# Padding the two rings of split weights by 64 and 96 bytes a buffer in a two-layer encoder kernel

## The chip, the cores and the metric

The kernel runs on one core of one Trainium2 chip. The metric is the device time of one execution in microseconds (us). Before the change three runs gave a median of 1837.78 us (1837.69 to 1837.85).

## The reference, cut to what matters

Two layers over 256 frames of width 1024, all in float32. Each layer has a mixer (layer 0: latent attention, "mla"; layer 1: sparse attention with a top-k indexer, "dsa"), a layer norm, an expert channel mixer ("peer") and another layer norm. Nearly all of the arithmetic is in the peer part: of 16384 experts it needs, for each frame, the product with their down rows, a gelu, a gate, and the sum of their up rows.

```python
def per_block(args):
    x_blk, e_blk, g_blk = args
    u = w_down[e_blk]
    a = jnp.einsum('td,ted->te', x_blk, u).astype(jnp.float32)
    hg = (jax.nn.gelu(a, approximate=False) * g_blk).astype(w_up.dtype)
    return jnp.einsum('te,ted->td', hg, w_up[e_blk]).astype(x_blk.dtype)
...
for i in range(DEPTH):
    m = _mla_mixer(...) if i % N_MIXERS == 0 else _dsa_mixer(...)
    x = _layernorm(DN_ALPHA * x + m, ln_gain[i, 0], ln_bias[i, 0])
    f = _peer(x, peer_w_q[i], peer_sub_keys[i], peer_w_down[i], peer_w_up[i])
    x = _layernorm(DN_ALPHA * x + f, ln_gain[i, 1], ln_bias[i, 1])
```

## The kernel before

The kernel doesn't gather experts. It multiplies the frames with the down rows of all 16384 experts, sets a gate that is zero for those not chosen, and multiplies with all up rows. So the weights go through the core once, as 128x1024 float32 blocks (4096 bytes in each of the 128 partitions). `Stream` (L52 to L131) feeds them: SyncE's queue loads a block into one of four `raw` buffers (L77), ScalarE copies it, rounded to float32r, into one of four `hi` buffers (L96), and VectorE writes the remainder raw - hi, float32r too, into one of four `lo` buffers (L100; a few on GpSimd, L98). `open` and `close` (L110 to L127) do the same with the subtraction set later, and `first` (L1142) does block 0 by hand with `hi0` and `lo0` from L1133 and L1134. `get` keeps three blocks split ahead of the one in use, and three more loaded.

The frames are split in the same way into `xh` and `xl` (128 x 8 x 256 float32r each). Every product of a frame chunk with a weight chunk is three float32r matmuls, high by high, low by high and high by low (`mm3`, L258). TensorE is the only engine that does them, all at L253 (`mm`). An operand that stands still in the array is loaded ahead of each matmul (LDWEIGHTS, "PEld" in the profile), while the one before still runs; the other operand moves through it. Three shapes matter here:

- **256 columns, weights stand still** (`proj`, L264): the group `d` (the peer's down product, twice 128 blocks of 24 matmuls), `pq` (the peer's queries), `q` and `qi` (dsa's), `h`, `krope` and `kn` (mla's). The weights are a slice of 128 columns (512 bytes) of a hi or lo buffer, and a 256-column chunk (1024 bytes) of `xh` or `xl` moves.
- **512 columns, weights move** (`rows`, L289): the group `y` (the peer's up product, twice 128 blocks of 12 matmuls, and the output projections), `v` and `qw`. Half of a hi or lo buffer (2048 bytes) moves, a slice of 128 columns of `xh` or `xl` stands still.
- **the exceptions**: `qn` and `qr` of mla (`up`, L745) move a 256-column float32r piece that lies in the tiles `V` and `U` (L721, L725) instead of `xh` and `xl`, and `ki` of dsa (L832) loads slices of only 72 columns, 288 bytes apart, from one hi and one lo buffer.

While the down product runs, VectorE, ScalarE and GpSimd choose the experts (`choose`, from L995) and build the gates (L1053 to L1059), and TensorE puts small matmuls `G` (L1068) between the blocks. The order on each engine comes from the order of the code and a scheduler.

SBUF is laid out by the order in which pools are opened (L167 to L176): `lead`, `wide` (xh, xl), `raws`, `his`, `los`, `big` (the arena), `const`, `small`, `ohp` (V and U). In the program as built, the first bytes of the buffers in each partition are, before:

| buffers | first byte | past a multiple of 512 |
|---|---|---|
| xh, xl | 17408, 25600 | 0, 0 |
| raw, four | 33792, 37888, 41984, 46080 | 0 |
| hi, four | 50176, 54272, 58368, 62464 | 0 |
| lo, four | 66560, 70656, 74752, 78848 | 0 |
| arena | 82944 | 0 |
| V, two; U, two | 220352, 222400; 224448, 226496 | 192 |

Of the kernel before, what the change touches and what calls it, by code (L numbers as in the profile page):

```python
# [11 lines left out]
F32R = mybir.dt.float32r  # L12
# [6 lines left out]
P = 128  # L19
T = 256  # L20
D = 1024
# [23 lines left out]
WARM = 9  # L45
EARLY = 11264
GSCALE = 2.0 ** 14
DSA_POOL = 3
MAGIC = 12582912.0


class Stream:  # L52
# [13 lines left out]

    def add(self, src, w=D):
        self.blocks += [(src[i], w) for i in range(src.shape[0])]

    def _load(self, upto):  # L70
        while self.n_loaded <= min(upto, len(self.blocks) - 1):
            src, w = self.blocks[self.n_loaded]
            if self.n_loaded in self.early:
                t = self.early[self.n_loaded]
            else:
                t = self.raw.tile([P, D], F32, tag="raw", name=f"raw{self.n_loaded}")
                self.last = self.nc.sync.dma_start(t[:, :w], src).ins  # L77
            self.tiles.append(t)
            self.n_loaded += 1
# [8 lines left out]
    def _split(self, upto, pooled=False):  # L88
        nc = self.nc
        while self.n_split <= min(upto, len(self.blocks) - 1):  # L90
            w = self.blocks[self.n_split][1]
            self._load(self.n_split)
            raw = self.tiles[self.n_split][:, :w]
            hi = self.hi.tile([P, D], F32R, tag="hi", name=f"hi{self.n_split}")[:, :w]
            lo = self.lo.tile([P, D], F32R, tag="lo", name=f"lo{self.n_split}")[:, :w]
            self.act(lambda: nc.scalar.copy(hi, raw))  # L96
            if pooled or self.share and self.n_split % self.share == 0:
                nc.gpsimd.tensor_tensor(lo, raw, hi.bitcast(F32), op=ALU.subtract)  # L98
            else:
                self.dve(lambda: nc.vector.tensor_tensor(lo, raw, hi.bitcast(F32), op=ALU.subtract))  # L100
            self.ready.append((hi, lo))
            self.n_split += 1
# [7 lines left out]
    def open(self, queue):  # L110

        i = self.n_split
        assert i == self.n_taken
        self._load(i)
        raw = self.tiles[i]
        hi = self.hi.tile([P, D], F32R, tag="hi", name=f"hi{i}")
        lo = self.lo.tile([P, D], F32R, tag="lo", name=f"lo{i}")
        queue("act", lambda: self.nc.scalar.copy(hi, raw))
        self.ready.append((hi, lo))
        self.n_split += 1  # L120
        self.n_taken += 1
        return i
# [39 lines left out]
def tile_trunk(ctx: ExitStack, tc: tile.TileContext, ins, out: bass.AP):  # L162
    nc = tc.nc
    def pool(name, bufs, **kw):
        return ctx.enter_context(tc.tile_pool(name=name, bufs=bufs, **kw))
# [4 lines left out]
    his = pool("his", 4)  # L170
    los = pool("los", 4)
# [41 lines left out]
    ws = Stream(nc, raws, his, los)  # L213
# [593 lines left out]
    def dsa():  # L807
# [82 lines left out]
        for t in range(2):  # L890
            for n in range(2):
                nc.scalar.copy(v[:, t, n * 512 : (n + 1) * 512], v4[t][n])
        ws.share = DSA_POOL
        for h in range(0, HEADS, 2):
# [22 lines left out]
    def peer(li):  # L917
# [77 lines left out]
        def choose():  # L995
# [40 lines left out]
            gt, i1 = tail[:, 0:T], tail[:, T : 2 * T]  # L1036
            nc.vector.tensor_scalar(gt, pg[:, :T], GSCALE, None, op0=ALU.mult)
            nc.vector.tensor_copy(gate16, gt)
# [23 lines left out]
        def place(g4, done):  # L1062
# [8 lines left out]
            if done < P:  # L1071
                nc.scalar.mul(A[:, done:, tsl], pv[:, done:, :], 1.0 / GSCALE)
            if done:
                nc.vector.scalar_tensor_tensor(A[:, :done, tsl], pv[:, :done, :], 1.0 / GSCALE, A[:, :done, tsl],
                                               op0=ALU.mult, op1=ALU.mult)
# [54 lines left out]
    xt = Arena(arena, 30720).take(NC, T)  # L1130
    piece = [slice(c, c + 2) for c in range(0, NC, 2)]
    raw0 = raws.tile([P, D], F32, tag="raw", name="raw0")
    hi0 = his.tile([P, D], F32R, tag="hi", name="hi0")  # L1133
    lo0 = los.tile([P, D], F32R, tag="lo", name="lo0")  # L1134
    nc.sync.dma_start(raw0, ins["mla_h"][0])
    for c in range(0, NC, 4):
        last = nc.sync.dma_start(xt[:, c : c + 4, :], ins["xT"][c // 4])
# [135 lines left out]
```

## Time and profile before

The profiled execution has a span of 1836.6 us; around it lie 1.2 us to the median of the runs.

| what | value |
|---|---|
| median of three runs | 1837.78 us |
| span of the profiled execution | 1836.6 us |
| mean granted TensorE clock | 0.999 |
| TensorE busy (matmuls) | 1824.8 us, 99% |
| VectorE, ScalarE, GpSimd busy | 1317.8, 1056.2, 362.8 us |
| moved by DMA | 335.47 MB, mean 183 GB/s |

A busy row of TensorE counts a matmul from its start until its result has left the array, so rows of neighbouring matmuls overlap: the mean ns of one matmul is longer than the distance between two starts. That distance (the pitch, below) is what the time is made of, and it is read from the chain of work that ended last (a piece's time by its count) or from starts in the order of time.

### The profile page before, as it was taken

Reading aid. Unit: us, or ns where it says so; the run is one execution under the profiler, and the core shown is the slowest. Engines: PE = TensorE matmul, PEld = TensorE weight load, DVE = VectorE, ACT = ScalarE, POOL = GpSimd, SP = SyncE. Lnnn points to the kernel's source line nnn. Section 1 sums busy time; section 2 is a strip of 40 time slices with the busy share of each in tenths; the row PEclk is TensorE's granted clock in tenths of the full one; section 3 lists DMA queues with packets and bytes.
Section 4 is the critical chain, followed back from the end, with each engine's and each line's share of the span. In section 5 each row is a group of like instructions: output and inputs, shape, how many; then the busy total and the mean of one; then the engine's idle time right before and its main releaser. Section 6 shows DMA issues by size and latency. Waiting matters only on the chain.

```text
span 1836.6 us, 32394 instructions
## 1 busy us (share of the span) xinstructions
PE 1824.8 (99%) x12495; PEld 1671.9 (91%) x12495; DVE 1317.8 (72%) x2348; ACT 1056.2 (58%) x1834; POOL 362.8 (20%) x265
## 2 busy tenths in 40 slices
PE   9999999999999999999999999999999999999998
PEld 8899999999998888888889899999999988888886
DVE  6689986788865555555688789957888765555555
ACT  6655456887764444444466555548877654444443
POOL 2002442445510000000022004504455300000000
PEclk9999999999999999999999999999999999999999
DMA  7554555444456555555646445554444475555553
GB/s 240 195 179 167 184 184 172 162 161 152 161 174 237 192 192 194 193 194 195 210 157 227 164 165 182 173 193 161 154 157 155 168 235 192 194 193 194 195 195 116
DMA packets 93468, 335.47 MB, mean 183 GB/s; under 512 B 10368, under 2 KB 11392, under 8 KB 93312
## 3 DMA queue, kind: packets, MB, share of 16 engines
q1 hardware_dynamic: 93024, 332.87, 52.9%
q8 instruction: 98, 1.61, 0.4%
q14 instruction: 58, 0.48, 0.1%
q10 hardware_dynamic: 288, 0.52, 0.1%
HBM read 329.16 MB, written 4.19 MB: 182 GB/s over the span
## 4 chain that ended last, share of the span: by engine, by line
PE 98%; DVE 1%; issue 1%; ACT 0%; DMA 0%; SPq 0%; DVEq 0%; POOLq 0%; POOL 0%; ACTq 0%
PE d L253 40%; PE y L253 40%; PE pq L253 4%; PE G L253 3%; PE q L253 3%; PE v L253 1%; PE qw L253 1%; PE s L253 1%; PE ps L253 1%; PE h L253 1%; PE qi L253 1%; PE o L253 1%; PE qn L253 0%; DMA arena<-in_xT 0%; PE kn L253 0%
## 5 line engine op out<-in xcount | busy, mean ns | idle before, releaser
L100 DVE TENSOR_TENSOR lo<-raw,hi 128x1024 fp32r<-128x1024 f32 (+1 forms) x579 | 763.9, 1321 | 345.0 <-ACT hi L96 344.1
L96 ACT CAST hi<-raw 128x1024 fp32r<-128x1024 f32 (+1 forms) x583 | 611.0, 1049 | 561.7 <-PE d L253 265.3
L253 PE MATMUL d<-xh,hi 128*128 128x256 f32 x2048 | 585.1, 286 | 0.0
L253 PE MATMUL d<-xh,lo 128*128 128x256 f32 x2048 | 579.2, 283 | 0.0
L253 PE MATMUL d<-xl,hi 128*128 128x256 f32 x2048 | 579.2, 283 | 0.0
L253 PEld LDWEIGHTS d<-xl,hi 128*128 128x128 f32 x2048 | 392.7, 192 | 0.0
L253 PEld LDWEIGHTS d<-xh,lo 128*128 128x128 f32 x2048 | 392.6, 192 | 0.0
L253 PEld LDWEIGHTS d<-xh,hi 128*128 128x128 f32 x2048 | 392.5, 192 | 0.0
L253 PE MATMUL y<-lo,xh 128*128 128x512 f32 x1088 | 337.7, 389 | 0.0
L253 PE MATMUL y<-hi,xh 128*128 128x512 f32 x1088 | 337.7, 390 | 0.0
L253 PE MATMUL y<-hi,xl 128*128 128x512 f32 x1088 | 337.3, 389 | 0.0
L1055 POOL TENSOR_TENSOR gate<-hot,gate 128x512 f16<-128x512 f16 x128 | 221.8, 1751 | 310.6 <-DVE hot L1053 310.6
L253 PEld LDWEIGHTS y<-lo,xh 128*128 128x128 f32 x1088 | 204.2, 188 | 42.7 <-DVE lo L100 0.3
L253 PEld LDWEIGHTS y<-hi,xl 128*128 128x128 f32 x1088 | 204.2, 188 | 42.4
L253 PEld LDWEIGHTS y<-hi,xh 128*128 128x128 f32 x1088 | 203.8, 188 | 41.8
L347 POOL TENSOR_TENSOR st<-st,mhalf 128x1 f32<-128x1 f32 x8 | 4.4, 551 | 827.2 <-DVE st L345 827.2
L1059 ACT ACTIVATE gate<-hot,rest 128x128 f16<-128x128 f16 x512 | 166.1, 413 | 0.9 <-DVE hot L1053 0.9
L1114 ACT CAST xh<-arena 128x512 fp32r<-128x512 f32 x128 | 79.8, 623 | 145.6 <-PE y L253 145.4
L1115 DVE TENSOR_TENSOR xl<-arena,xh 128x512 fp32r<-128x512 f32 x128 | 88.2, 692 | 73.5 <-ACT xh L1114 73.5
L1053 DVE TENSOR_TENSOR hot<-iota,place 128x1024 f16<-128x1024 f16 x128 | 84.9, 703 | 49.1 <-PE G L253 49.0
L1024 POOL TENSOR_TENSOR arena<-arena 128x800 f32<-128x800 f16 x32 | 78.8, 2482 | 38.8 <-DVE arena L1022 38.0
L253 PE MATMUL G<-gate,hot 128*128 128x128 f16 x1024 | 70.1, 221 | 0.0
(222 smaller groups left out, 1739.5 us busy)
## 6 DMA issues: line engine op xcount, KB each, us to landing
raw<-in_down SPq DMA_DIRECT2D x256, 512.0 KB, 3.2
raw<-in_up SPq DMA_DIRECT2D x256, 512.0 KB, 4.3
raw<-in_peer_q SPq DMA_DIRECT2D x24, 512.0 KB, 4.4
raw<-in_dsa_qk SPq DMA_DIRECT2D x16, 512.0 KB, 3.2
raw<-in_mla_w_o SPq DMA_DIRECT2D x8, 512.0 KB, 5.9
arena<-in_peer_q SPq DMA_DIRECT2D x8, 512.0 KB, 4.3
raw<-in_dsa_v SPq DMA_DIRECT2D x8, 512.0 KB, 4.3
raw<-in_dsa_w_o SPq DMA_DIRECT2D x8, 512.0 KB, 3.7
```

Source lines behind the costliest of these rows:

```text
L96: self.act(lambda: nc.scalar.copy(hi, raw))
L100: self.dve(lambda: nc.vector.tensor_tensor(lo, raw, hi.bitcast(F32), op=ALU.subtract))
L253: return pe(lambda: nc.tensor.matmul(o, l, r, start=start, stop=stop, skip_group_check=True))
L347: nc.gpsimd.tensor_tensor(st[:, 5:6], st[:, 4:5], mhalf, op=ALU.pow)
L1024: nc.gpsimd.tensor_tensor(o.rearrange("p k c -> p c k"), same, cell[t][:, h, :, None].to_broadcast([P, CELLS, TOPK]), op=ALU.mult)
L1053: nc.vector.tensor_tensor(hot, iota4[:, None].to_broadcast([P, 2, P, 4]), place16[:, :, None, four].to_broadcast([P, 2, P, 4]), op=ALU.is_ ...
L1055: nc.gpsimd.tensor_tensor(gate[:, 0], hot[:, 1].rearrange("p c j -> p j c"), gate16[:, four, None].to_broadcast([P, 4, P]), op=ALU.mult)
L1059: nc.scalar.mul(gate[:, 1, j, :], hot[:, 1, :, j], rest[:, t : t + 1])
L1114: nc.scalar.copy(hh, a)
L1115: nc.vector.tensor_tensor(al, a, hh.bitcast(F32), op=ALU.subtract)
```

## The change

Each buffer of the hi ring gets 16 more float32 columns (64 bytes), each of the lo ring 24 (96 bytes). The code uses the first 1024 columns only. `parts` allots both in one place for the three places that did so apart.

```diff
+HI_PAD, LO_PAD = 16, 24
...
+    def parts(self, i, w=D):
+
+        hi = self.hi.tile([P, D + HI_PAD], F32R, tag="hi", name=f"hi{i}")
+        lo = self.lo.tile([P, D + LO_PAD], F32R, tag="lo", name=f"lo{i}")
+        return hi[:, :w], lo[:, :w]
...
-            hi = self.hi.tile([P, D], F32R, tag="hi", name=f"hi{self.n_split}")[:, :w]
-            lo = self.lo.tile([P, D], F32R, tag="lo", name=f"lo{self.n_split}")[:, :w]
+            hi, lo = self.parts(self.n_split, w)
...
-        hi = self.hi.tile([P, D], F32R, tag="hi", name=f"hi{i}")
-        lo = self.lo.tile([P, D], F32R, tag="lo", name=f"lo{i}")
+        hi, lo = self.parts(i)
...
-    hi0 = his.tile([P, D], F32R, tag="hi", name="hi0")
-    lo0 = los.tile([P, D], F32R, tag="lo", name="lo0")
+    hi0, lo0 = ws.parts(0)
```

On every engine the instructions stand in the same order as before, row for row, with the same waits. Only addresses move:

| buffers | first byte after | past a multiple of 512 |
|---|---|---|
| xh, xl, raw | as before | 0 |
| hi, four | 50176, 54336, 58496, 62656 | 0, 64, 128, 192 |
| lo, four | 66816, 71008, 75200, 79392 | 256, 352, 448, 32 |
| arena | 83584 | 128 |
| V, two; U, two | 220992, 223040; 225088, 227136 | 320 |

## The prediction

> **What bounds the kernel now.** I read the page first: its busy times, the granted clock and the chain of work that ended last.
>
> ```profile
> PE 1824.8 (99%) x12495; PEld 1671.9 (91%) x12495; DVE 1317.8 (72%) x2348; ACT 1056.2 (58%) x1834; POOL 362.8 (20%) x265
> ...
> PEclk9999999999999999999999999999999999999999
> ...
> PE 98%; DVE 1%; issue 1%; ACT 0%; DMA 0%; SPq 0%; DVEq 0%; POOLq 0%; POOL 0%; ACTq 0%
> ```
>
> 98% of the chain is TensorE, at full clock from end to end. So the time is the sum of the distances between the starts of its matmuls. Two pieces of the chain, in its order of time (start, length, matmuls), give that pitch:
>
> ```profile
> 151.56 146.63 PE d L253 x1222
> ...
> 548.60 348.19 PE y L253 x1536
> ```
>
> 146.63 us over 1222 is 120.0 ns for a 256-column matmul; 348.19 over 1536 is 226.7 ns for a 512-column one. 256 more columns cost 106.7 ns. Columns alone would therefore make 106.7 and 213.3 ns, and both kinds pay 13.3 ns on top. A change that touches neither the number of matmuls nor any wait of TensorE can win only from these 13.3 ns, or add to them.
>
> Does that surcharge depend on where operands lie? I grouped matmuls by tile, first in stretches in which TensorE had long been running (160 to 290 us, then 600 to 890 us; the last column but one is the mean ns of one matmul):
>
> ```profile
> L253 PE MATMUL d<-xh,hi 128*128 128x256 f32 x362 | 102.4, 283 | 0.0
> L253 PE MATMUL d<-xl,hi 128*128 128x256 f32 x362 | 102.4, 283 | 0.0
> L253 PE MATMUL d<-xh,lo 128*128 128x256 f32 x362 | 102.4, 283 | 0.0
> ```
>
> ```profile
> L253 PE MATMUL y<-hi,xl 128*128 128x512 f32 x428 | 131.7, 389 | 0.0
> ```
>
> In these, all operands begin at multiples of 512 bytes. All three products of d take 283 ns, though the other engines come and go during them (busy times by stretch: sum, then PE, PEld, DVE, ACT, POOL):
>
> ```profile
> 160.00:290.00 130.00, 130.00 (x1086) 130.00 (x1085) 111.45 (x332) 64.73 (x75) 49.93 (x48) 1.00 0.54 186
> ...
> 560.00:890.00 330.00, 330.00 (x1457) 273.26 (x1456) 188.96 (x180) 157.29 (x179) 0.00 (x0) 1.00 0.58 197
> ```
>
> So the surcharge isn't a collision with what VectorE, ScalarE, GpSimd or the DMA do; it would not be so even. It lies between TensorE's two own reads, the moving operand and the next weights. The few matmuls whose operands do not lie so, `qn` and `qr`, show another time (min/median/max ns; V lies 192 past a multiple of 512):
>
> ```profile
> L253 PE MATMUL qn<-V,hi x24: 276/276/367, 25.9 to 34.3; 128*128 128x256 f32 x24
> ...
> L253 PE MATMUL qn<-V,lo x24: 276/276/280, 26.2 to 34.5; 128*128 128x256 f32 x24
> ...
> L253 PE MATMUL qr<-V,hi x12: 281/281/367, 35.0 to 38.9; 128*128 128x256 f32 x12
> ...
> L253 PE MATMUL qr<-V,lo x12: 281/281/283, 35.3 to 39.2; 128*128 128x256 f32 x12
> ```
>
> That a shorter duration is a shorter pitch too, the starts say, beside the chain's piece:
>
> ```profile
> 30.54 4.21 PE qn L253 x36
> ```
>
> ```profile
> 31.08 0.28 PE L253 MATMUL qn<-V,lo 128*128 128x256 f32 x1
> ```
>
> ```profile
> 34.48 0.28 PE L253 MATMUL qn<-V,lo 128*128 128x256 f32 x1
> ```
>
> Between the sixth and the last of these 36 qn lie 3.40 us for 30 matmuls, 113.3 ns: 6.7 less than d, as 276 is 7 less than 283. And `ki`, with its usual `xh` and `xl` but weight slices that begin at eight different places (72 columns every 288 bytes), runs between them:
>
> ```profile
> L253 PE MATMUL ki<-xh,lo 128*72 128x256 f32 x8 | 2.2, 280 | 0.0
> L253 PE MATMUL ki<-xh,hi 128*72 128x256 f32 x7 | 2.0, 280 | 0.0
> L253 PE MATMUL ki<-xl,hi 128*72 128x256 f32 x7 | 2.0, 279 | 0.0
> ```
>
> So every 256-column float32r group whose two operands do not share their place past a multiple of 512 bytes is shorter than 283 ns: 276, 281 and 280. But qn and qr have the same offset and differ by 5 ns, so the offset alone does not fix the value. That is the weak point of what follows.
>
> **The change, part by part.** *The instructions.* None is added, removed or moved, and no wait changes: cost nothing, with no cover needed. *The splits.* ScalarE's copy and VectorE's subtraction now write, and VectorE reads, at other places:
>
> ```profile
> L100 DVE TENSOR_TENSOR lo<-raw,hi 128x1024 fp32r<-128x1024 f32 (+1 forms) x579 | 763.9, 1321 | 345.0 <-ACT hi L96 344.1
> L96 ACT CAST hi<-raw 128x1024 fp32r<-128x1024 f32 (+1 forms) x583 | 611.0, 1049 | 561.7 <-PE d L253 265.3
> ```
>
> I take no change. No row has them at another offset, so bounds come from elsewhere: in the stretch from 160 us VectorE is busy 111.45 of 130 us and TensorE never stops, so the subtraction (1321 ns of a block's 24 x 120.0 = 2880 ns) could grow by half of the 18.55 us left, some 200 ns for each of the 45 blocks there, before TensorE would notice. If it got faster, that would be worth nothing: TensorE doesn't wait for it. If that cover were gone, each 100 ns more would cost 579 x 0.1 = 58 us.
>
> *Places that are not multiples of 64.* The second and fourth lo buffers begin 32 bytes past one. The nearest row: mla's attention operands lie 20 bytes past a multiple of 64 (five floats are taken ahead of them in the arena), dsa's on one. The score matmuls of both, mla first:
>
> ```profile
> L253 PE MATMUL s<-arena x64: 270/326/382, 49.2 to 63.9; 128*128 128x128 f32 x32, 128*128 128x256 f32 x32
> ```
>
> ```profile
> L253 PE MATMUL s<-arena x32: 270/378/382, 977.0 to 998.1; 128*128 128x128 f32 x16, 128*128 128x256 f32 x16
> ```
>
> The same shortest and longest (the medians mix two sizes): nothing, though these are plain float32.
>
> *The 256-column matmuls.* Their weights come from four buffers in turn. The first hi stays where it was and the first lo is 256 past a multiple of 512; I give that pair no gain. The other three hi lie 64, 128 and 192 past, their lo 352, 448 and 32, against `xh` and `xl` at 0. The counts (pq and q have three such groups each, like d):
>
> ```profile
> L253 PE MATMUL d<-xh,hi 128*128 128x256 f32 x2048 | 585.1, 286 | 0.0
> L253 PE MATMUL d<-xh,lo 128*128 128x256 f32 x2048 | 579.2, 283 | 0.0
> L253 PE MATMUL d<-xl,hi 128*128 128x256 f32 x2048 | 579.2, 283 | 0.0
> ...
> L253 PE MATMUL y<-lo,xh 128*128 128x512 f32 x1088 | 337.7, 389 | 0.0
> ```
>
> ```profile
> L253 PE MATMUL pq<-xh,lo 128*128 128x256 f32 x192 | 54.8, 285 | 0.0
> ...
> L253 PE MATMUL q<-xh,hi 128*128 128x256 f32 x128 | 36.9, 288 | 0.0
> ```
>
> 3 x (2048 + 192 + 128) = 7104, three quarters of them 5328. The gain of one lies between 7 ns (qn) and 0 (no effect of these offsets); the three rows average (276 + 281 + 280) / 3 = 279, and I take 4 ns. 5328 x 4 = **21.3 us less**, bounds 37.3 and 0.
>
> *The 512-column matmuls.* Here the weights move, 3 x 1088 = 3264 of them, 2448 from the three shifted buffers. No row shows one at another offset. The equal surcharge of 13.3 ns suggests the same relief (7 ns: 17.1 us less; 4 ns: 9.8). Against it speaks how they settle: the first ones after the change of shape, from 548.4 to 549.9 us are slower than the 389 to which they come.
>
> ```profile
> L253 PE MATMUL y<-hi,xh 128*128 128x512 f32 x4 | 1.3, 394 | 0.0
> L253 PE MATMUL y<-lo,xh 128*128 128x512 f32 x3 | 1.0, 391 | 0.0
> ```
>
> If shifted buffers kept them from settling, each would cost up to 394 - 389 = 5 ns more: 12.2 us. Between -17.1 and +12.2 I take 0, since the two hints point opposite ways.
>
> *The sum.* 1836.6 - 21.3 = 1815.3 us of span. The 1.2 us around it stay, which makes **1816.5 us** against the median of 1837.78.
>
> **The rivals.** *Full relief.* All shifted buffers behave as qn: 37.3 + 17.1 = 54.4 us less, **1783.4**. For it: qn holds 276 over two batches, whatever buffer its weights are in. Against it: qr and ki.
>
> *Nothing.* The short pitch of qn is due to V's lying far from hi, or to something in mla that I don't see: **1837.8**. For it: qr differs from qn at equal offsets. Against it: ki uses `xh`, `xl` and the ring as d does. A rule of the Trainium skill would give this result too. "TensorE: Matmul & The Clock Gate", section "Step-by-step: what each phase is for", gives TensorE two independent read ports, so that loading the next weights takes nothing from the running matmul; by that rule no offset between the two could matter. The same page's section "Wait — 56ns, not 53.3ns?" puts the pitch at the columns over 2.4 GHz plus some 2.5 ns, an estimate of 109.2 ns here; the trace's 120.0 does not agree, and 113.3 in one place and 120.0 in another speaks against the rule.
>
> *Slower.* One mechanism: the 512-column matmuls have their best value, 389, only because all operands share their offset, and shifted buffers leave them unsettled at 394, while the 256-column ones gain nothing: 12.2 us more, **1850.0**. It decides once the 256-column gain is below 12.2 / 5328 = 2.3 ns, about what qr (281 against 283) has. For it: the two rows above. Against it: the few slow ones follow a change of shape, which the ring doesn't bring.
>
> *VectorE as the bound* stays out: even full relief takes 54.4 us off 1836.6, 3%, and in its densest long stretch VectorE has 18.55 of 130 us free, 14%.
>
> **How the numbers follow.** Forecast 0.42 (own range 1801 to 1833: below, 5 ns on the 256-column side and -9.8 on the other; above, 2 ns and half of the +12.2), full relief 0.20, nothing 0.18, slower 0.20. Faster by over 0.2% (3.7 us, about what a measurement of this kernel can tell from no change): 0.62; within: 0.18; slower: 0.20. The range reaches down to full relief, 1783, and up to 1845, where the slower case is half way with a gain of 1 ns on the 256-column side; about 2 in 10 stay outside. The likeliest is 1816.5.
>
> **What would show it.** In the profile after, right: the piece of d from about 152 us is shorter by some 3 ns a matmul on average, with the blocks of one buffer in four still at 283 ns, three at 276 to 281, and the y piece within 5 ns of 389. Wrong: d at 283 throughout (nothing), y above 392 (slower), d and y both 5 ns or more shorter (full relief), or new idle time of TensorE behind L96 or L100, which no part of this argument has.

## The result, and the profile after

Timed side by side, before took 1837.74 us (1837.69 to 1837.85) and after 1847.42 us (1847.07 to 1847.68). The ratio is 1.0051, with an interval of 1.0039 to 1.0063: the change makes the kernel slower by 0.5%. The forecast was 1816.5, the range ended at 1845, and the slower rival stood at 1850.0. The profiled execution after has a span of 1845.4 us against 1836.6, 8.8 more.

The page shows the same kernel as before: the same counts, VectorE, ScalarE and GpSimd busy as before, full clock, TensorE 98% of the chain.

```profile
PE 1834.0 (99%) x12495; PEld 1664.6 (90%) x12495; DVE 1317.4 (71%) x2348; ACT 1055.0 (57%) x1834; POOL 362.8 (20%) x265
...
PEclk9999999999999999999999999999999999999999
...
PE 98%; DVE 1%; issue 0%; ACT 0%; DMA 0%; SPq 0%; DVEq 0%; POOLq 0%; POOL 0%; ACTq 0%
...
L106 DVE TENSOR_TENSOR lo<-raw,hi 128x1024 fp32r<-128x1024 f32 (+1 forms) x579 | 763.6, 1321 | 350.4 <-ACT hi L102 349.4
L102 ACT CAST hi<-raw 128x1024 fp32r<-128x1024 f32 (+1 forms) x583 | 610.0, 1047 | 564.2 <-PE d L258 259.2
```

L253, L96 and L100 of before are L258, L102 and L106 here. The splits take 1047 and 1321 ns, as before (1049 and 1321), and no idle time of TensorE behind them is new. So the time went into the matmuls' own distances. The chain in its order of time (start, length, matmuls) has the same two pieces in each layer:

```profile
151.14 145.51 PE d L258 x1222
544.46 356.05 PE y L258 x1536
1087.50 145.55 PE d L258 x1222
1481.91 350.00 PE y L258 x1510
```

145.51 / 1222 is 119.1 ns where before had 120.0: a gain of 0.9 ns for a 256-column matmul. 356.05 / 1536 is 231.8 ns where before had 226.7: 5.1 ns more for a 512-column one. The second layer repeats both. The groups by tile, from 160 to 290 us and from 600 to 890 us (the last column but one is the mean ns of one matmul, 283 and 389 before), say the same:

```profile
L258 PE MATMUL d<-xl,hi 128*128 128x256 f32 x365 | 102.9, 282 | 0.0
L258 PE MATMUL d<-xh,lo 128*128 128x256 f32 x365 | 102.9, 282 | 0.0
L258 PE MATMUL d<-xh,hi 128*128 128x256 f32 x364 | 102.7, 282 | 0.0
```

```profile
L258 PE MATMUL y<-lo,xh 128*128 128x512 f32 x418 | 131.2, 395 | 0.0
L258 PE MATMUL y<-hi,xl 128*128 128x512 f32 x417 | 130.3, 393 | 0.0
L258 PE MATMUL y<-hi,xh 128*128 128x512 f32 x418 | 130.3, 393 | 0.0
```

I counted the distance from each start to the next over all matmuls of d and y in both traces (gaps left out): d goes from 119.90 to 118.83 ns, y from 226.75 to 231.79. With the prediction's counts this is 7104 x -1.07 = -7.6 us and 3264 x +5.04 = +16.5 us, together +8.9; the span grew by 8.8. Those two terms are the whole growth of the span. The other 0.9 us of the 9.7 lie around it: 2.0 us between span and median here, 1.1 before.

### The profile page after: what moved, and what is told of

Its sections match the earlier page's. It is cut to its first block, busy times and chain, and to the rows that moved or that the text cites. A ratio compares the mean times of both kernels' runs of the same rounds, so it can differ in the third digit from the quotient of the medians.

```text
span 1845.4 us, 32394 instructions
## 1 busy us (share of the span) xinstructions
PE 1834.0 (99%) x12495; PEld 1664.6 (90%) x12495; DVE 1317.4 (71%) x2348; ACT 1055.0 (57%) x1834; POOL 362.8 (20%) x265
## 4 chain that ended last, share of the span: by engine, by line
PE 98%; DVE 1%; issue 0%; ACT 0%; DMA 0%; SPq 0%; DVEq 0%; POOLq 0%; POOL 0%; ACTq 0%
PE y L258 41%; PE d L258 40%; PE pq L258 4%; PE G L258 3%; PE q L258 3%; PE v L258 1%; PE qw L258 1%; PE s L258 1%; PE ps L258 1%; PE h L258 1%; PE qi L258 1%; PE o L258 1%; PE qn L258 0%; DMA raw<-in_mla_h 0%; PE kn L258 0%
## 5 line engine op out<-in xcount | busy, mean ns | idle before, releaser
L106 DVE TENSOR_TENSOR lo<-raw,hi 128x1024 fp32r<-128x1024 f32 (+1 forms) x579 | 763.6, 1321 | 350.4 <-ACT hi L102 349.4
L102 ACT CAST hi<-raw 128x1024 fp32r<-128x1024 f32 (+1 forms) x583 | 610.0, 1047 | 564.2 <-PE d L258 259.2
L258 PE MATMUL d<-xh,hi 128*128 128x256 f32 x2048 | 582.9, 285 | 0.0
L258 PE MATMUL d<-xl,hi 128*128 128x256 f32 x2048 | 576.3, 281 | 0.0
L258 PE MATMUL d<-xh,lo 128*128 128x256 f32 x2048 | 576.1, 281 | 0.0
L258 PEld LDWEIGHTS d<-xh,lo 128*128 128x128 f32 x2048 | 387.9, 189 | 0.0
L258 PEld LDWEIGHTS d<-xh,hi 128*128 128x128 f32 x2048 | 386.8, 189 | 0.0
L258 PEld LDWEIGHTS d<-xl,hi 128*128 128x128 f32 x2048 | 386.4, 189 | 0.0
L258 PE MATMUL y<-lo,xh 128*128 128x512 f32 x1088 | 344.2, 395 | 0.0
L258 PE MATMUL y<-hi,xl 128*128 128x512 f32 x1088 | 342.1, 393 | 0.0
L258 PE MATMUL y<-hi,xh 128*128 128x512 f32 x1088 | 341.9, 393 | 0.0
L258 PEld LDWEIGHTS y<-hi,xl 128*128 128x128 f32 x1088 | 204.3, 188 | 48.9
L258 PEld LDWEIGHTS y<-lo,xh 128*128 128x128 f32 x1088 | 204.3, 188 | 47.2 <-DVE lo L106 0.3
L258 PEld LDWEIGHTS y<-hi,xh 128*128 128x128 f32 x1088 | 203.7, 188 | 47.0
L258 PE MATMUL G<-gate,hot 128*128 128x128 f16 x1024 | 70.2, 221 | 0.0
```

The source lines that it names most:

```text
L258: return pe(lambda: nc.tensor.matmul(o, l, r, start=start, stop=stop, skip_group_check=True))
```

## The experiments

Two theories stood at the start. **A, own offset:** a matmul's distance depends on the offset between the operand that moves and the weights that are loaded meanwhile, and the best offset of one width isn't that of the other. **B, unsettling:** it is the change of offset from buffer to buffer that costs; any one constant offset is as good as the old one. An offset below is the first byte of the operand that stands (is loaded) minus that of the one that moves, modulo 256 (why 256, the third group of experiments shows). A ring buffer 64 bytes later has thus offset 64 in d, where it stands, and 192 in y, where it moves. By this count `qn` of before lay at 64, as d does in `u64`; the expectation of `u192` puts it at that kernel's offset, which is not so. Before, on the chips of these runs, took 1838.31 us (first four kernels), 1838.26 (`split64`, `split8`) and 1838.05 (the last four).

### One pad alone

`hi_only` is after with

```diff
-HI_PAD, LO_PAD = 16, 24
+HI_PAD, LO_PAD = 16, 0
```

> The change's pads of 64 on the hi ring alone; the lo buffers then all lie 256 past a multiple of 512. Theory A: the hi rows of the padded kernel (d 119.9, 118.4, 119.4, 117.6; y 229.8, 230.8, 231.0, 233.3) and the lo row at 256 (119.6; 233.0): d and the like about -6 us, y about +16 us: 1848 us. Theory B: hi and lo differ in every product, so about as the change: 1844 to 1850 us.

`lo_only` is after with

```diff
-HI_PAD, LO_PAD = 16, 24
+HI_PAD, LO_PAD = 0, 24
```

> The change's pads of 96 on the lo ring alone, hi as before at 0, lo at 0, 96, 192 and 288. Theory A: the hi matmuls at 0 have their old pitch (120.0 and 226.7), and only the lo third pays, 3264/3 x 0.75 x 6 ns = +5 us at most and some -2 us in d: 1839 to 1842 us. Theory B: three blocks in four change offset twice in every product, also for their hi matmuls: y 229 to 232, 1842 to 1849 us; the fourth block only pays until it has settled.

Measured: 1841.73 us, ratio 1.0018 (1.0009 to 1.0028), and 1841.36 us, 1.0016 (1.0007 to 1.0026). Each pad alone costs about a third of what both cost. For `hi_only` both theories had said too much (1848, and 1844 to 1850); `lo_only` lies inside A's range and just under B's. The pieces of the chain, `hi_only` first:

```profile
151.22 144.78 PE d L258 x1222
543.95 354.55 PE y L258 x1536
```

```profile
151.42 145.15 PE d L258 x1222
545.04 353.35 PE y L258 x1536
```

Both sides of the balance are there in each: d gains (118.5 and 118.8 ns), y pays (230.8 and 230.0). `lo_only` also shows who pays. In it every hi buffer is where it was before; only three of four lo buffers are shifted. Mean distance by product and offset, counted from starts (ns; before 226.75 throughout):

```
y<-lo,xh  offset 0: 227.3   160: 233.0   64: 232.7   224: 233.4
y<-hi,xh  offset 0: 229.0   (never shifted)
y<-hi,xl  offset 0: 229.8   (never shifted)
```

The shifted products pay 6 to 7 ns, as A has it. But the unshifted ones, which alternate with them, pay 2 to 3 as well: a part of B is true. In after it is a larger part. Its products at offset 0 are those of the first hi (232.3 with xh, 227.2 with xl) and of the first lo, 256 past a multiple of 512 (233.0), on average 4.1 ns over 226.75; the nine at other offsets pay 5.4, and one of them, the second hi with xh, only 1 (227.7).

### One offset for all eight buffers

`u64` is before with a gap ahead of the rings, so that all eight buffers begin 64 bytes later and nothing changes from buffer to buffer. `u192` has 48 columns there, 192 bytes.

```diff
+    pool("gap", 1).tile([P, 16], F32, tag="gap", name="gap")
     his = pool("his", 4)
```

> No pads; the whole hi and lo rings begin 64 bytes later, so all eight buffers share one offset (64) to xh and xl. Theory A (own offset): a matmul has the pitch that goes with its own offset, whatever its neighbours do; in the padded kernel the buffers at 64 have 118.4 ns in d (119.9 before) and 230.8 in y (226.8 before), so 7104 x -1.5 = -10.7 us and 3264 x +4.0 = +13.1 us: 1840 us. Theory B (unsettling): what costs is that the offset changes from one matmul to the next, and a ring of one offset settles to one value: no more than 1838 us, and if it settles as qn did before (6.7 ns less a matmul, 10368 of them) 1768 us.

> As u64 with 192 bytes. Theory A: the buffer at 192 in the padded kernel has 117.6 ns in d and 233.3 in y: 7104 x -2.3 = -16.3 us and 3264 x +6.5 = +21.2 us: 1843 us. Theory B: one settled value, no more than 1838 us, and 1768 us if as qn, whose V lay at this offset to hi.

Measured: 1839.66 us, ratio 1.0008 (0.9998 to 1.0017), and 1840.03 us, 1.0009 (1.0000 to 1.0019). The chain of `u64`, and its y from 600 to 890 us:

```profile
149.23 143.93 PE d L254 x1222
539.16 358.40 PE y L254 x1536
```

```profile
L254 PE MATMUL y<-lo,xh 128*128 128x512 f32 x416 | 131.2, 397 | 0.0
```

The total hardly moves, but both pieces do: d falls to 117.8 ns and y rises to 233.3, more than in after. `u192` has the same lengths, 143.93 and 358.41 us. So B falls as the main cause: with one constant offset y pays the most of all. A holds where the offset is constant; among buffers at several offsets, the neighbours have a say too. A's 1840 for `u64` came true by luck: d gained 2.4 ns and not 1.5, y paid 6.4 and not 4.0. Its 1843 for `u192` was 3 us too much. In all these one-offset kernels the weights of a matmul and those loaded while it runs lie at the same offset, so they don't tell which of the two counts.

### The matmuls alone

Can TensorE do this with the core's other engines idle? `bench` leaves out all layers and copies x to the output; it was run once, like `fine` below. It runs 36 matmuls at each offset, upward and then downward, 256 and then 512 columns, weights and moving operand in two tiles:

```diff
+            s = still_at // 4 + 128 * (k % 8)
+            m = moved_at // 4 + n * (k % (1024 // n))
+            nc.tensor.matmul(p[:, :n], still[:, s : s + P], moved[:, m : m + n], start=k == 0, stop=k == count - 1)
...
+    places = list(range(0, 512, 32)) + [16, 8]
```

> Not the reference's computation: it leaves all layers out, copies x to the output and runs float32r matmuls alone, with no other engine beside them. 36 in a row for each distance in place, past a multiple of 512 bytes, of the standing operand to the moving one: 0 to 480 in steps of 32, then 16 and 8, upward and then downward, with 256 and then with 512 columns; last both operands at 64, then both at 192. Own offset: each group settles after a few matmuls to one pitch, the same upward and downward; 0 gives 120.0 and 226.7 ns, 64 and 192 give 117.6 and 233.2, and the groups with both operands moved alike give what 0 gives. Neighbours: a group's value depends on the side it is entered from. Other engines: if the surcharge came from what they do, all groups would lie near 107 and 213 ns here.

`fine` is the same with a step of 4 bytes.

```diff
-    places = list(range(0, 512, 32)) + [16, 8]
+    places = list(range(0, 256, 4))
```

> As the matmul-only kernel before (all layers left out, x copied to the output), with the standing operand 0, 4, 8 ... 252 bytes past the moving one, 36 matmuls each, 256 columns and then 512. Own offset: the multiples of 32 give again what they gave, to 1 ns where a group had one value both ways (256 columns: 120.0, 118.6, 117.8, 117.3, 118.5, about 119.9, 117.7; 512: 226.7, 233.4, 233.4, 234.3, 232.9, 233.1, 228.8, 233.2), and 8 gives 115.6 and 230.6. If 8 is no single exception, other small offsets lie below 117 ns with 256 columns too. Neighbours or chance: values that repeat nowhere.

The page of `bench`: VectorE, ScalarE and GpSimd are busy for under 5 us of 504.2 together.

```profile
PE 494.9 (98%) x2796; PEld 431.8 (86%) x2796; DVE 1.4 (0%) x2; ACT 3.2 (1%) x2; POOL 0.2 (0%) x4
```

Its chain has one piece of 36 matmuls for each offset (upa 0, upc 64, upg 192, upi 256, upq and dnq 16, dnp 480, dnh 224; bothq has both operands at 192), first with 256 columns, from 186.57 us with 512:

```profile
24.63 4.31 PE upa L79 x36
33.20 4.24 PE upc L79 x36
50.26 4.24 PE upg L79 x36
58.74 4.31 PE upi L79 x36
109.69 4.32 PE dnp L79 x36
143.88 4.20 PE dnh L79 x36
182.26 4.32 PE bothq L79 x36
186.57 8.21 PE upa L79 x36
203.18 8.40 PE upc L79 x36
236.76 8.24 PE upg L79 x36
253.40 8.17 PE upi L79 x36
320.18 8.16 PE upq L79 x36
344.94 8.40 PE dnq L79 x36
495.22 8.16 PE bothq L79 x36
```

Three things are to be seen. With both operands moved alike (bothq) it is 120.0 and 226.7 ns, the kernel's old values: what counts is the offset between the two. At 256 it is as at 0 (upi beside upa), and the seven other pairs of upward rows that lie 256 apart agree to 0.01 us in both widths: the period is 256 bytes. And the two widths have opposite signs: at 64, 4.24 / 36 = 117.8 ns is 2.2 under the old value, and 8.40 / 36 = 233.3 is 6.6 over it. These are the values of `u64`'s d (offset 64) and `u192`'s y (64 as well). One value of the kernels differs: `u64`'s y has offset 192 and took 233.3 ns, where `bench` has 8.24 / 36 = 228.9. Of the 512-column offsets in steps of 32 bytes, 0 (with 256) is the cheapest; of the 256-column ones it is the dearest, together with 160 (rows not shown; 119.7 to 120.1 ns).

Something is left beside the offset: upq and dnq have the same offset of 16 bytes and take 226.7 and 233.3 ns; dnp and dnh, 256 bytes apart, take 120.0 and 116.7. `fine` has more of this: 64 and 192 (fcs, fgs), 117.8 in `bench`, take 113.6 and 113.3 here, and 204 (fgv) takes more than offset 0 (fas). At the other multiples of 32, and with 512 columns at all of them, `fine` repeats the upward rows of `bench` to about 1 ns. The last line is 204 with 512 columns, 226.7 ns: there the dearest offset of one width is as cheap as 0 is in the other. (So are 120, 144, 156 and 252 with 512 columns; rows not shown.)

```profile
24.65 4.31 PE fas L79 x36
...
92.56 4.09 PE fcs L79 x36
...
228.76 4.08 PE fgs L79 x36
241.32 4.43 PE fgv L79 x36
...
723.37 8.16 PE fgv L79 x36
```

So an offset has more than one value to which a row of matmuls can settle. Which of them it takes depends on more than the offset. Rows that go upward and downward differ in what ran before, but also in the PSUM buffer that they write; dnp and dnh write the same one as the program is built, so the buffer alone doesn't decide. Nor does the chip: `fine` and `split64` (below) ran on the same one, and 64 bytes took 113.6 ns in the first and 117.8 in the second. What ran before is the likeliest, but no run isolates it.

### The two widths apart

If A is right, gain and loss can be had separately. `split64` is before with two views of the frames' tiles: the projections (256 columns) read theirs from byte 192, so that the weights lie 64 past them modulo 256; the up product and the output projections read theirs from byte 0. The writers of the frames (L689, L822 and L1113 of before) write to whichever view is read next.

```diff
+    wh = wide.tile([P, NC * T + 64], F32R, tag="xh", name="xh")
+    wl = wide.tile([P, NC * T + 64], F32R, tag="xl", name="xl")
+    xh, xl = [w[:, 48 : 48 + NC * T].rearrange("p (c t) -> p c t", t=T) for w in (wh, wl)]
+    yh, yl = [w[:, : NC * T].rearrange("p (c t) -> p c t", t=T) for w in (wh, wl)]
...
-        oh, ol = xh, xl
+        oh, ol = yh, yl
```

> No pads on the rings. The tiles of xh and xl are 256 bytes longer; the projections use them from byte 192 on, the y matmuls and the output projections from byte 0. So only matmuls with standing weights get an offset (weights 64 past the moving chunk, in multiples of 256), and y keeps 0. Own offset: 7104 x (117.8 - 120.0) = -15.6 us, y unchanged, some 1 us back in the few v and qw matmuls that read the shifted view: 1823 us. Rival, place of the rings themselves: they did not move, so no change: 1838 us.

`y64` is the reverse: projections at 0, the 512-column products' view from byte 64 (the edit against `split64`).

```diff
-    xh, xl = [w[:, 48 : 48 + NC * T].rearrange("p (c t) -> p c t", t=T) for w in (wh, wl)]
-    yh, yl = [w[:, : NC * T].rearrange("p (c t) -> p c t", t=T) for w in (wh, wl)]
+    xh, xl = [w[:, 0 : 0 + NC * T].rearrange("p (c t) -> p c t", t=T) for w in (wh, wl)]
+    yh, yl = [w[:, 16 : 16 + NC * T].rearrange("p (c t) -> p c t", t=T) for w in (wh, wl)]
```

> The other half of the split alone: the projections use xh and xl from byte 0 as before, the y matmuls and the output projections from byte 64 on, no pads on the rings. Own offset: the matmul-only kernels gave 233.2 to 233.5 ns for 512 columns at 64, so 3264 x +6.6 = +21.5 us: 1860 us, and d stays at 120.0. Rival, the price of y in the padded kernel came from the change of offset between hi, lo and the buffers: one offset for all costs nothing: 1838 us.

Measured: `split64` 1818.76 us (1816.84 to 1819.69), ratio 0.989 (0.9874 to 0.9907), 19.5 us less and 4 under what was expected; `y64` 1859.51 us, 1.0116 (1.0099 to 1.0133), 21.5 us more. The chains, `split64` first:

```profile
149.80 143.93 PE d L255 x1222
539.73 348.21 PE y L255 x1536
```

```profile
152.00 146.63 PE d L255 x1222
549.04 358.40 PE y L255 x1536
```

`split64` has the d of `u64` with the y of before; `y64` has the d of before with the y of `u192`, whose offset it shares. The two changes, -19.5 and +21.5, add up to +2.0 us; `u64`, which has the same d and a y that pays as much (at 192), measured +1.4. Gain and loss are separate, each follows its own offset, and in `u64` they cancel.

### Other offsets for the projections

Can more be had? Four kernels are `split64` with the projections' view from another byte: 64 (`split192`), 248 (`split8`), 168 (`split88`) and 204 (`split52`); the number in the name is where the weights then lie. Once settled, rows of `bench` or `fine` had shown 117.7 or 113.4 ns there (192), 115.6 (8), 113.4 (88) and 113.4 (52).

```diff
-    xh, xl = [w[:, 48 : 48 + NC * T].rearrange("p (c t) -> p c t", t=T) for w in (wh, wl)]
+    xh, xl = [w[:, 16 : 16 + NC * T].rearrange("p (c t) -> p c t", t=T) for w in (wh, wl)]
```

> As split64, with the projections' view from byte 64 on (weights 192 past the moving chunk). The matmul-only kernels gave 117.7 in one, 113.4 in the other. Own offset with one value: 117.6, as split64: 1819 us. If the offset allows two values and this program comes into the lower: 113.4, 7104 x -6.6 = -47 us: 1791 us.

> As split64, but the projections use xh and xl from byte 248 on, so the weights lie 8 past the moving chunk. Own offset: 115.6 ns in the matmul-only kernel, 7104 x -4.4 = -31 us, 1 us back: 1808 us. Rival, the other engines' work spoils the fine value: at or above split64, 1823 us or more. Rival, place of the rings: 1838 us.

> As split64, from byte 168 on (weights 88 past). The fine matmul-only kernel gave 113.4 ns here: 1791 us if the full kernel comes into the same value. As in the kernel with 8, where the matmul-only 115.6 became 120.1, it may not: then 117 to 120 ns, 1817 to 1838 us.

> As split64, from byte 204 on (weights 52 past). The fine matmul-only kernel gave 113.4 ns: 1791 us if it carries over; else 117 to 120 ns, 1817 to 1838 us.

Measured: `split192` 1817.91 us, ratio 0.9891 (0.9875 to 0.9908), the lowest median of this study, though the runs of `split64` spread around it; `split8` 1840.36 us, 1.0011 (1.0002 to 1.0021); `split88` 1839.45 us, 1.0008 (0.9998 to 1.0017); `split52` 1828.7 us, 0.9949 (0.9932 to 0.9965). The pieces of d, of `split192`, `split8`, `split88` and `split52` in turn:

```profile
150.53 143.93 PE d L255 x1222
```

```profile
151.73 146.65 PE d L255 x1222
```

```profile
151.13 146.64 PE d L255 x1222
```

```profile
151.45 143.93 PE d L255 x1222
```

At 8 and 88 bytes d is at 120.0 ns, as at offset 0; what the matmuls alone had shown there didn't carry over, and the hope for 113 ns fell; `split8` is 32 us over the 1808 expected. Whether the other engines spoil such a value, the rival named there, isn't shown; `qn` of before held 113.3 ns with VectorE busy for 4.6 and ScalarE for 5.7 of 7.9 us (26.5 to 34.4). At 52 this piece is 117.8 ns, but d as a whole, counted from starts, is at 118.3. At 64 and 192 the kernel keeps to 117.8 in this piece and to 117.5 and 117.0 as a whole.

## Why the prediction was wrong

**What held.** No instruction and no wait moved; the splits cost what they did; TensorE alone sets the time; and the surcharge lies between TensorE's two own reads, whatever the other engines do. `bench` shows the last point with those engines idle. It also settles the first doubt of the rival "nothing": 120.0 at one offset and 117.8 at another, with all else equal, isn't something in mla. The Trainium skill's rule of two independent read ports ("TensorE: Matmul & The Clock Gate", section "Step-by-step: what each phase is for") doesn't agree with these rows.

**The step that failed: the 512-column term, taken as 0.** It measured +16.5 us. The prediction had two hints of opposite sign and put itself between them. The 512-column matmuls of before were already at the lowest value (no offset in `bench` or `fine` settled below 226.6 ns), so a shift could only cost or change nothing; the hint of relief came from assuming that the equal surcharge of 13.3 ns has the same cure in both widths. `bench` shows it hasn't: with 512 columns the surcharge is smallest at offset 0, and 6.6 ns more at 64.

Even the upper bound of that term, 12.2 us, was too low. Its 5 ns a matmul happens to be the average that was measured; its count was wrong. It charged 2448 matmuls and spared those of the first buffer. In after the first hi and the first lo pay 4.1 ns on average, though their offset is 0; `lo_only` shows the same where hi never moves.

**The second step: 4 ns for each shifted 256-column matmul, 21.3 us.** It measured 7.6 us, 1.07 ns averaged over all 7104. Direction right, size a third. The three rows behind the 4 ns were qn (276), qr (281) and ki (280), and the plain mean let the exceptional 276 pull. A constant offset of 64 gives 117.5 (2.4 ns), near qr's row. The pads gave less, since 128 brought little (119.6 and 119.2 for the third hi's two products) and the first hi nothing (119.7 and 120.1). That qn and qr differ at one offset, named as the weak point, is what `bench` and `fine` show in the open: an offset can settle at more than one value. From their starts in before, qn took 113.3 ns and qr 117.7, the two values of offset 64 in `fine` and `bench`.

**The rivals.** "Slower" had the right side and half of the mechanism: the 512-column matmuls have their best value because their operands share their offset; its sign, y above 392 ns, came (393 to 395). The other half, that shifted buffers keep them from settling, is true in part at most: at a constant offset they settle, at 233.3 ns, and pay 6.6. Its time of 1850.0 against 1847.42 is near by luck, from two errors that partly cancel: no gain from the 256-column side (it was 7.6 us), and 12.2 for the other (it was 16.5). Its point of decision, a 256-column gain below 2.3 ns, was worked out with that low price. "Full relief" fell on the y side and "nothing" on both.

The same two terms, with the distances counted from starts in each trace, against what was measured:

| kernel | d, ns | y, ns | 7104 x d + 3264 x y, us | measured, us |
|---|---|---|---|---|
| after | -1.07 | +5.04 | -7.6 + 16.5 = +8.9 | +9.7 (span +8.8) |
| `hi_only` | -1.41 | +4.08 | -10.0 + 13.3 = +3.3 | +3.4 |
| `lo_only` | -1.13 | +3.37 | -8.0 + 11.0 = +3.0 | +3.0 |
| `y64` | 0.0 | +6.55 | +21.4 | +21.5 |
| `u64` | -2.42 | +6.41 | -17.2 + 20.9 = +3.7 | +1.4 |
| `u192` | -2.77 | +6.58 | -19.7 + 21.5 = +1.8 | +1.7 |
| `split64` | -2.38 | +0.05 | -16.9 + 0.2 = -16.7 | -19.5 |
| `split192` | -2.88 | +0.02 | -20.5 + 0.1 = -20.4 | -20.1 |

Six of the eight kernels come out within 1 us. `u64` and `split64` are 2 to 3 us lower than the two terms. The 7104 leave out h, qi, kn and krope, 288 more matmuls of 256 columns: in the trace of `u64` these take 2.0 us less than in before. In `split64` h and qi take 1.3 us less, and its median lies 0.9 us under the run that was profiled.

**What stays open.** Why each pad alone costs 3 us and both 9.7: the offsets of neighbouring matmuls matter (in after, 4.1 ns for products at offset 0), but no run isolates how. What in the memory or in TensorE has a period of 256 bytes, and why an offset can settle at more than one value, no run here tells.

## What to carry to other kernels

Where TensorE never waits, read the distance between starts from long pieces of the chain, one shape at a time; an excess over what the columns explain may hang on where the two operands begin. Here float32r matmuls of 512 columns wanted both operands at one place modulo 256 bytes, and those of 256 columns wanted them 64 or 192 apart, so at these offsets one buffer used in both roles can't serve both: give the other operand two views (`split64`, `split192`: 1.1% faster) and don't pad the ring. (In `fine` the frames 204 bytes past the ring would have served both, 226.7 ns with 512 columns and, the ring then standing at 52, 113.4 with 256; no kernel tried that, and in `split52` the offset of 52 gave 118.3.) Try such an offset in the kernel itself, for a value that a row of matmuls shows by itself need not come with it (8 and 88 bytes).

## What the runs showed of the hardware that was not expected

- The distance between float32r matmuls depends on the offset between the two operands with a period of 256 bytes, and the two widths respond in opposite ways: 120.0 ns at 0 and 117.8 at 64 with 256 columns, 226.7 and 233.3 with 512.
- It does so with the other engines idle (under 5 of 504.2 us busy in `bench`), so it isn't contention with them.
- One offset can settle at two values: 16 bytes at 226.7 and 233.3 ns (`bench`, upward and downward), 64 bytes at 117.8 (`bench`, `split64`) and 113.6 (`fine`); 192 bytes with 512 columns at 228.9 (`bench`) and 233.3 (`u64`).
- An unshifted matmul among shifted ones pays as well: 229.0 and 229.8 against 226.75 ns (`lo_only`), 232.3, 227.2 and 233.0 (after).
